# Token expansion by expert weights: all token loads and all stores on SyncE's DMA queue, the two weight loads on ScalarE's

## The chip, the cores and the metric

The kernel runs on one core of a Trainium2 chip; the chip's other cores run nothing. The metric is the device time of one execution in microseconds (us), as the median of several executions of the same program. Less is better. The profiled execution is one more run, under the hardware profiler; its page gives a span, which begins at the program's first own instruction and ends with its last, and is a little shorter than the device time of the same run.

## What is computed

Every token row of 512 floats is written twice, each time multiplied by one of that token's two weights. The expert indices are an input that the computation doesn't use.

```python
batch, seq, hidden, n_experts = 16, 1024, 512, 8      # k = 2
x_expanded = x[:, :, np.newaxis, :].repeat(k, axis=2)  # [16, 1024, 2, 512]
weights = expert_weights[..., np.newaxis]              # [16, 1024, 2, 1]
return (x_expanded * weights).astype(np.float32)
```

There are 16384 tokens, 33.55 MB of x to read, 0.13 MB of weights to read, and 67.11 MB of output to write, all float32.

## The kernel before, in words

**Tiling.** The 16384 tokens are 128 x 128: `groups = [19, 19, 18, 18, 18, 18, 18]` cuts them into seven groups of 128 x T tokens, and a partition holds T neighbouring tokens. So a group's load is one long contiguous run per partition (18 x 2048 = 36,864 bytes), and a store of 9 tokens with two products each is 9 x 4096 = 36,864 bytes per partition.

**Loads.** `load(i)` (L120) takes a buffer of `x_pool`, which has two, and starts the DMA of group i at L128. Group 0 is loaded in two DMAs (9 and 10 tokens), every other group in one. Groups 0 and 1 are loaded ahead of the loop; at the end of its iteration i the loop calls `load(i + 2)`, whose buffer is that of group i.

**Products.** A group is worked off in two halves (j = 0 and 1), each into a buffer of `o_pool`, which has three. `products` (L134) has one long VectorE instruction (L135) that multiplies up to nine tokens by both weights, and, in one half of each group, ScalarE does the two products of one further token (L148). In every group but the first it is half 0 in which ScalarE helps, in the first group half 1. Each half is followed by its store (L172). There are 14 stores, here S0 to S13; the loads are L0a, L0b, L1, L2 to L6. S(2i) and S(2i+1) are the two stores of group i.

**Weights.** The weights have to stand in `w_tile` with a token on its partition. They come in with two small DMAs (`weights_in`, L72): `raw_a`, 38 KB for groups 0 and 1, and `raw_b`, 90 KB for groups 2 to 6. TensorE transposes them twice (L87, L98) and VectorE copies the results (L92, L106). The `raw_a` chain comes ahead of the loop; that of `raw_b` stands in the loop ahead of the second half of group 0, and its last copy after that half.

**Order.** The schedule is manual: each engine executes its instructions in the order in which the program calls them, and waits come only from data and buffers. A DMA that is started from SyncE or from ScalarE is put on that engine's queue. Before, SyncE's queue (q1 in the profile) has `raw_a` and the 14 stores; ScalarE's queue (q10) has L0a, L0b, `raw_b`, L1, and then L2 to L6, each of which stands in ScalarE's program behind the ScalarE products of the group before. A store waits for its products; a load waits until the products that read its buffer are done; products wait for their load and for the store that was three stores earlier, whose buffer they take.

Of the kernel before, what the change touches and what calls it, by code (L numbers as in the profile page):

```python
# [1 line left out]

# [4 lines left out]


@with_exitstack
def kernel(  # L10
    ctx: ExitStack,
    tc: tile.TileContext,
    x: bass.AP,
    expert_indices: bass.AP,
    expert_weights: bass.AP,
    out: bass.AP,
):
    nc = tc.nc

    batch, seq, hidden = x.shape  # L20
    k = expert_weights.shape[-1]
    P = nc.NUM_PARTITIONS
    ntok = batch * seq
    assert ntok % P == 0

    f32 = mybir.dt.float32
    row = k * hidden


    groups = [19, 19, 18, 18, 18, 18, 18]  # L30
    assert sum(groups) * P == ntok
    TX = max(groups)
    TO = (TX + 1) // 2

    xf = x.rearrange("b s h -> (b s) h")
    of = out.rearrange("b s k h -> (b s) (k h)")
    wf = expert_weights.rearrange("b s k -> (b s) k")

    w_pool = ctx.enter_context(tc.tile_pool(name="w_pool", bufs=1))
    x_pool = ctx.enter_context(tc.tile_pool(name="x_pool", bufs=2))  # L40
    o_pool = ctx.enter_context(tc.tile_pool(name="o_pool", bufs=3))

    raw_pool = ctx.enter_context(tc.tile_pool(name="raw_pool", bufs=1))
    psum = ctx.enter_context(
        tc.tile_pool(name="psum", bufs=2, space=bass.MemoryType.PSUM)
    )

    w_tile = w_pool.tile([P, sum(groups) * k], f32)

    def rows(flat, done, T):  # L50
        return flat[done * P : (done + T) * P, :].rearrange("(p a) n -> p (a n)", a=T)

    B = 8
    M = P // B
    ident = w_pool.tile([P, P], f32)
    nc.gpsimd.memset(ident, 0.0)  # L59
    nc.gpsimd.affine_select(  # L60
        out=ident,
        in_=ident,
        compare_op=mybir.AluOpType.not_equal,
        fill=1.0,
        base=0,
        pattern=[[-1, P]],
        channel_multiplier=1,
    )

    def weights_in(eng, head, G, T):  # L70
        raw_tile = raw_pool.tile([G * M, B * T * k], f32, name=f"raw{T}_tile")
        eng.dma_start(  # L72
            out=raw_tile,
            in_=wf[head * P : (head + G * T) * P, :].rearrange(
                "(q a) n -> q (a n)", a=B * T
            ),
        )
        return raw_tile

    def weights_columns(raw_tile, G, T):  # L80
        n = T * k
        col_tile = raw_pool.tile([n, G * P], f32, name=f"col{T}_tile")
        cols = col_tile.rearrange("c (q r) -> c q r", r=B)
        for r0 in range(0, B, B // 2):
            up_tile = psum.tile([n, B // 2, G * M], f32)
            for r in range(B // 2):
                nc.tensor.transpose(  # L87
                    up_tile[:, r, :],
                    raw_tile[:, (r0 + r) * n : (r0 + r + 1) * n],
                    ident[: G * M, : G * M],  # L90
                )
            nc.vector.tensor_copy(  # L92
                out=cols[:, :, r0 : r0 + B // 2],
                in_=up_tile.rearrange("c r q -> c q r"),
            )
        down_tile = psum.tile([P, G * n], f32)
        for g in range(G):
            nc.tensor.transpose(  # L98
                down_tile[:, g * n : (g + 1) * n],
                col_tile[:, g * P : (g + 1) * P],  # L100
                ident[:n, :n],
            )
        return down_tile

    def weights_out(down_tile, head, G, T):
        nc.vector.tensor_copy(  # L106
            out=w_tile[:, head * k : (head + G * T) * k], in_=down_tile
        )

    ctx.enter_context(tc.manual_schedule())  # L110

    starts = [sum(groups[:i]) for i in range(len(groups))]
    loaded = []


    def halves(i):
        T = groups[i]
        return [T - T // 2, T // 2] if i else [T // 2, T - T // 2]

    def load(i):  # L120
        if i >= len(groups):
            return
        x_tile = x_pool.tile([P, TX * hidden], f32)
        loaded.append(x_tile)
        src = rows(xf, starts[i], groups[i])
        lo = 0
        for n in halves(i) if i == 0 else [groups[i]]:
            nc.scalar.dma_start(  # L128
                out=x_tile[:, lo * hidden : (lo + n) * hidden],
                in_=src[:, lo * hidden : (lo + n) * hidden],  # L130
            )
            lo += n

    def products(o_tile, x_tile, at, n, w_at, m):  # L134
        nc.vector.tensor_tensor(  # L135
            out=o_tile[:, : m * row].rearrange("p (t k h) -> p t k h", t=m, k=k),
            in0=x_tile[:, at * hidden : (at + m) * hidden]
            .rearrange("p (t h) -> p t h", t=m)
            .unsqueeze(2)
            .to_broadcast([P, m, k, hidden]),  # L140
            in1=w_tile[:, w_at : w_at + m * k]
            .rearrange("p (t k) -> p t k", t=m)
            .unsqueeze(3)
            .to_broadcast([P, m, k, hidden]),
            op=mybir.AluOpType.mult,
        )
        for c in range(m * k, n * k):
            nc.scalar.mul(  # L148
                out=o_tile[:, c * hidden : (c + 1) * hidden],
                in_=x_tile[:, (at + c // k) * hidden : (at + c // k + 1) * hidden],  # L150
                mul=w_tile[:, w_at + c : w_at + c + 1],
            )

    raw_a = weights_in(nc.sync, starts[0], 2, 19)
    load(0)
    raw_b = weights_in(nc.scalar, starts[2], 5, 18)
    load(1)
    weights_out(weights_columns(raw_a, 2, 19), starts[0], 2, 19)

    for i, T in enumerate(groups):  # L160
        x_tile = loaded[i]
        outr = rows(of, starts[i], T)
        at = 0
        for j, n in enumerate(halves(i)):
            if i == 0 and j == 1:
                down_b = weights_columns(raw_b, 5, 18)
            o_tile = o_pool.tile([P, TO * row], f32)

            alone = j == 1 and i > 0 or j == 0 and i == 0
            m = n if alone else n - 1  # L170
            products(o_tile, x_tile, at, n, (starts[i] + at) * k, m)
            nc.sync.dma_start(  # L172
                out=outr[:, at * row : (at + n) * row], in_=o_tile[:, : n * row]
            )
            at += n
        if i == 0:
            weights_out(down_b, starts[2], 5, 18)
        load(i + 2)

# [1 line left out]
_INS = ['x', 'expert_indices', 'expert_weights']  # L181
_OUTS = [((16, 1024, 2, 512), 'float32')]


# [23 lines left out]
```

## Time and profile before

| | before |
|---|---|
| device time, median of 3 runs | 240.32 us (239.97 to 240.71) |
| device time of the profiled execution | 241.2 us |
| span of the profiled execution | 239.4 us |
| bytes moved by DMA | 100.80 MB, 3312 packets |
| mean rate over the span | 421 GB/s |
| SyncE's queue q1: packets, MB, share of the 16 DMA engines' span | 2064, 67.15, 65.0% |
| ScalarE's queue q10: the same | 1248, 33.65, 33.1% |
| VectorE busy | 133.0 us (56%) |
| ScalarE busy | 10.6 us (4%) |

The profile counts DMA work in packets; a packet here is what one partition gets or gives in one DMA. There are 16 DMA engines, and the share of a queue is the time of its packets, added up over the engines, as a share of 16 times the window. In a view of a short window a packet is counted where it starts, so that the share of a very short window can be above 1. The times from issue to landing hold the waiting in the queue as well as the moving. The profile's views don't tell the 16 DMA engines apart.

### The profile page before, as it was taken

The page shows a single profiled execution, that of the slowest core. Times are in us where ns is not written, and L with a number is a line of the kernel's source. Part 1 is how long each engine was busy: PE and PEld are TensorE (multiplying, and loading weights), DVE is VectorE, ACT ScalarE, POOL GpSimd, SP SyncE. Part 2 cuts the span into 40 slices and gives each one's busy share as a digit, 9 for nine tenths or more (in the row PEclk, how much of TensorE's full clock was granted, in tenths as well). Part 3 has the DMA queues.
Part 4 walks back from the last instruction along what each step waited for, and adds up shares of the span by engine and source line. Part 5 has one row for each costly group of instructions (what it writes and reads, how often), then busy time and mean ns, then how long its engine had stood idle before and what let it go on. Part 6 is the DMA issues. An engine that isn't in the chain of part 4 may idle for free.

```text
span 239.4 us, 196 instructions
## 1 busy us (share of the span) xinstructions
PE 3.0 (1%) x23; PEld 2.3 (1%) x23; DVE 133.0 (56%) x20; ACT 10.6 (4%) x15; POOL 0.7 (0%) x6
## 2 busy tenths in 40 slices
PE   1021000000000000000000000000000000000000
PEld 1011000000000000000000000000000000000000
DVE  1499959890093088940872910789407839690000
ACT  0040020000010000100002000002000020000000
POOL 1000000000000000000000000000000000000000
DMA  7999999999999999999999999999999999999993
GB/s 268 440 444 380 449 394 474 435 416 427 406 471 450 422 419 431 450 400 468 413 437 450 394 474 413 425 462 394 468 419 425 456 400 468 413 431 456 400 468 129
DMA packets 3312, 100.80 MB, mean 421 GB/s; under 512 B 384, under 2 KB 496, under 8 KB 496
## 3 DMA queue, kind: packets, MB, share of 16 engines
q1 hardware_dynamic: 2064, 67.15, 65.0%
q10 hardware_dynamic: 1248, 33.65, 33.1%
HBM read 33.69 MB, written 67.11 MB: 421 GB/s over the span
## 4 chain that ended last, share of the span: by engine, by line
DMA 66%; DVE 24%; issue 0%; DVEq 0%; SPq 0%
DMA out_dram<-o_tile 62%; DVE o_tile L135 24%; DMA x_tile<-in_x_dram 3%; DVE col_tile L92 0%; DVEq L135 0%; SPq L172 0%
## 5 line engine op out<-in xcount | busy, mean ns | idle before, releaser
L135 DVE TENSOR_TENSOR o_tile<-x_tile,w_tile 128x9216 f32<-128x9216 f32 (+1 forms) x14 | 131.3, 9376 | 78.2 <-DMA out_dram<-o_tile 71.2
L148 ACT ACTIVATE o_tile<-x_tile,w_tile 128x512 f32<-128x512 f32 x14 | 9.3, 714 | 170.3 <-DMA out_dram<-o_tile 123.5
L92 DVE COPY col_tile<-up_tile 38x128 f32<-38x128 f32 (+1 forms) x4 | 1.4, 378 | 4.2 <-PE up_tile L87 4.2
L87 PE MATMUL up_tile<-ident,raw_tile 32*38 32x32 f32 (+1 forms) x16 | 1.8, 284 | 14.6 <-DMA raw_tile<-in_expert_weights_dram 14.6
L148 ACT ACT_TABLE_LOAD x1 | 1.3, 1283 | 15.5 <-DMA x_tile<-in_x_dram 15.5
L87 PEld LDWEIGHTS up_tile<-ident,raw_tile 32*38 32x38 f32 (+1 forms) x16 | 1.4, 134 | 14.7 <-issue 14.7
L98 PE MATMUL down_tile<-ident,col_tile 36*128 36x36 f32 (+1 forms) x7 | 1.2, 305 | 3.0 <-DVE col_tile L92 3.0
L98 PEld LDWEIGHTS down_tile<-ident,col_tile 36*128 36x128 f32 (+1 forms) x7 | 0.9, 209 | 3.4 <-DVE col_tile L92 3.4
L106 DVE COPY w_tile<-down_tile 128x76 f32<-128x76 f32 (+1 forms) x2 | 0.6, 282 | 0.5 <-PE down_tile L98 0.5
L60 POOL TENSOR_SCALAR_AFFINE_SELECT ident<-ident 128x128 f32<-128x128 f32 x1 | 0.3, 292 | 0.1
L59 POOL MEMSET ident<- 128x128 f32 x1 | 0.2, 205 | 0.3 <-POOLq L192 0.3
L192 POOL MEMSET const-bfloat16-1.0<- 128x1 bf16 x1 | 0.1, 101 | 0.0
L192 POOL MEMSET const-uint8-127<- 128x1 uint8 x1 | 0.1, 101 | 0.0
L192 POOL MEMSET const-float32-0.0<- 128x1 f32 x1 | 0.1, 98 | 0.2 <-issue 0.2
L192 POOL MEMSET const-float32-1.0<- 128x1 f32 x1 | 0.1, 98 | 0.0
## 6 DMA issues: line engine op xcount, KB each, us to landing
out_dram<-o_tile SPq DMA_DIRECT2D x12, 4608.0 KB, 35.5
x_tile<-in_x_dram ACTq DMA_DIRECT2D x5, 4608.0 KB, 26.1
out_dram<-o_tile SPq DMA_DIRECT2D x2, 5120.0 KB, 38.8
x_tile<-in_x_dram ACTq DMA_DIRECT2D x1, 4864.0 KB, 29.9
x_tile<-in_x_dram ACTq DMA_DIRECT2D x1, 2560.0 KB, 14.3
x_tile<-in_x_dram ACTq DMA_DIRECT2D x1, 2304.0 KB, 8.4
raw_tile<-in_expert_weights_dram ACTq DMA_DIRECT2D x1, 90.0 KB, 14.2
raw_tile<-in_expert_weights_dram SPq DMA_DIRECT2D x1, 38.0 KB, 2.9
```

Source lines behind the costliest of these rows:

```text
L59: nc.gpsimd.memset(ident, 0.0)
L60: nc.gpsimd.affine_select(out=ident, in_=ident, compare_op=mybir.AluOpType.not_equal, fill=1.0, base=0, pattern=[[-1, P]], channel_multipl ...
L87: nc.tensor.transpose(up_tile[:, r, :], raw_tile[:, (r0 + r) * n : (r0 + r + 1) * n], ident[: G * M, : G * M],)
L92: nc.vector.tensor_copy(out=cols[:, :, r0 : r0 + B // 2], in_=up_tile.rearrange("c r q -> c q r"),)
L98: nc.tensor.transpose(down_tile[:, g * n : (g + 1) * n], col_tile[:, g * P : (g + 1) * P], ident[:n, :n],)
L106: nc.vector.tensor_copy(out=w_tile[:, head * k : (head + G * T) * k], in_=down_tile)
L135: nc.vector.tensor_tensor(out=o_tile[:, : m * row].rearrange("p (t k h) -> p t k h", t=m, k=k), in0=x_tile[:, at * hidden : (at + m) * hidden]
L148: nc.scalar.mul(out=o_tile[:, c * hidden : (c + 1) * hidden], in_=x_tile[:, (at + c // k) * hidden : (at + c // k + 1) * hidden], mul=w_ti ...
L192: nc = _bacc.Bacc("TRN2", target_bir_lowering=False, num_devices=1)
```

## The change

Both weight loads are started from ScalarE, and `raw_b` ahead of the first token load; all token loads are started from SyncE, in whose program they stand between the stores.

```diff
@@ load(i)
         for n in halves(i) if i == 0 else [groups[i]]:
-            nc.scalar.dma_start(
+            nc.sync.dma_start(
                 out=x_tile[:, lo * hidden : (lo + n) * hidden],
                 in_=src[:, lo * hidden : (lo + n) * hidden],
             )
@@ ahead of the loop
-    raw_a = weights_in(nc.sync, starts[0], 2, 19)
+    raw_a = weights_in(nc.scalar, starts[0], 2, 19)
+    raw_b = weights_in(nc.scalar, starts[2], 5, 18)
     load(0)
-    raw_b = weights_in(nc.scalar, starts[2], 5, 18)
     load(1)
```

In the built program SyncE's queue then holds, in this order: L0a, L0b, L1, S0, S1, L2, S2, S3, L3, S4, S5, L4, S6, S7, L5, S8, S9, L6, S10, S11, S12, S13. ScalarE's queue holds `raw_a` and `raw_b` alone. The instructions of VectorE, TensorE and GpSimd stand in the order of before; ScalarE loses its token loads.

## Prediction

> **What bounds the kernel now.** I read the page's busy times first, then its DMA part and its chain.
>
> ```profile
> span 239.4 us, 196 instructions
> ...
> PE 3.0 (1%) x23; PEld 2.3 (1%) x23; DVE 133.0 (56%) x20; ACT 10.6 (4%) x15; POOL 0.7 (0%) x6
> ...
> DMA packets 3312, 100.80 MB, mean 421 GB/s; under 512 B 384, under 2 KB 496, under 8 KB 496
> ...
> q1 hardware_dynamic: 2064, 67.15, 65.0%
> q10 hardware_dynamic: 1248, 33.65, 33.1%
> ...
> DMA 66%; DVE 24%; issue 0%; DVEq 0%; SPq 0%
> ```
>
> The busiest compute engine, VectorE, has 56%; the two queues together keep the 16 DMA engines busy for 65.0 + 33.1 = 98.1% of 239.4 us, that is 234.9 us on average. The DVE share of the chain is therefore not a bound: while VectorE multiplies, DMA runs too. What the change can move is how long the 16 DMA engines take for the same 100.80 MB, and what stands ahead of and behind them.
>
> So I asked the DMA view for windows with one kind of traffic. Stores only, 188 to 234 us:
>
> ```profile
> DMA packets 607, 20.02 MB, mean 435 GB/s; under 512 B 64, under 2 KB 64, under 8 KB 64
> ...
> q1 hardware_dynamic: 607, 20.02, 100.7%
> ```
>
> 100.7% of 46 us is 46.3 us for 20.02 MB: 432 GB/s while busy. Token loads only, 5 to 13 us:
>
> ```profile
> DMA packets 192, 3.47 MB, mean 434 GB/s; under 512 B 16, under 2 KB 16, under 8 KB 16
> ...
> q10 hardware_dynamic: 192, 3.47, 100.9%
> ```
>
> 100.9% of 8 us, 8.07 us for 3.47 MB: 430 GB/s. And 33 to 188 us, where loads come and go beside stores:
>
> ```profile
> q1 hardware_dynamic: 1295, 43.48, 64.9%
> q10 hardware_dynamic: 720, 23.59, 35.3%
> ```
>
> 100.2% of 155 us is 155.3 us for 67.07 MB: 432 GB/s. The three kinds cost the same per byte, and no window leaves the engines idle. At 432 GB/s all 100.80 MB need 233.3 us, and 234.9 were used. Most of the 1.6 us too many lies in the first 30 us:
>
> ```profile
> DMA packets 608, 11.86 MB, mean 395 GB/s; under 512 B 64, under 2 KB 176, under 8 KB 176
> ...
> q10 hardware_dynamic: 512, 10.05, 81.9%
> q1 hardware_dynamic: 96, 1.81, 14.7%
> ```
>
> 96.6% of 30 us is 29.0 us, where 11.86 MB at 432 GB/s need 27.5: 1.5 us too many. The end of the span, by the windows view (last two columns: DMA share, GB/s):
>
> ```profile
> 234.00:234.50 0.50, 0.00 (x0) 0.00 (x0) 0.00 (x0) 0.00 (x0) 0.00 (x0) 1.00 0.51 221
> 234.50:235.00 0.50, 0.00 (x0) 0.00 (x0) 0.00 (x0) 0.00 (x0) 0.00 (x0) 1.00 2.22 958
> 235.00:235.50 0.50, 0.00 (x0) 0.00 (x0) 0.00 (x0) 0.00 (x0) 0.00 (x0) 1.00 0.00 0
> 235.50:236.00 0.50, 0.00 (x0) 0.00 (x0) 0.00 (x0) 0.00 (x0) 0.00 (x0) 1.00 0.18 74
> 236.00:236.50 0.50, 0.00 (x0) 0.00 (x0) 0.00 (x0) 0.00 (x0) 0.00 (x0) 1.00 0.01 0
> 236.50:237.00 0.50, 0.00 (x0) 0.00 (x0) 0.00 (x0) 0.00 (x0) 0.00 (x0) 1.00 0.17 74
> ```
>
> A store packet of 36.9 KB takes 36.9 KB / 27 GB/s = 1.36 us of one engine. 221 GB/s for half a us are three such packets, 958 are thirteen, 74 is one. So sixteen start up to 235.0, and then a single engine starts one more at 235.5 to 236 and its last at 236.5 to 237. Fifteen engines are done by 235.0 + 1.4 = 236.4; **one engine is about 2 us late**, and the kernel waits for it.
>
> **The change part by part.** All times are against the profiled execution: span 239.4 us, 1.8 us around it, 241.2 in all, 0.9 above the median of 240.32. I apply differences to the median.
>
> *Issues and their waits: 0.* The rows of before are these, from the timeline and SyncE's waits:
>
> ```profile
> 9.20 9.76 DVE L135 TENSOR_TENSOR o_tile<-x_tile,w_tile 128x9216 f32<-128x9216 f32 x1 [3.76 <-DMA x_tile<-in_x_dram]
> 18.99 10.85 SPq L172 DMA_DIRECT2D out_dram<-o_tile  x2
> 29.49 0.36 ACTq L128 DMA_DIRECT2D x_tile<-in_x_dram  x1
> 32.89 9.76 DVE L135 TENSOR_TENSOR o_tile<-x_tile,w_tile 128x9216 f32<-128x9216 f32 x1 [3.22 <-DMA x_tile<-in_x_dram]
> ...
> SPq L172 <- DVE o_tile L135: 191.7, 13, 21.4
> ```
>
> SyncE did nothing but wait for products (191.7 us of it), so eight more issues of about 0.36 us each cost nothing there. L(i+2) now stands behind S(2i+1) on SyncE, but both wait for the same products of group i: L2 went out at 29.49, with the second store. Queued behind the load is S(2i+2), whose products come some 9 us later. Where the built program makes SyncE wait for a landing, too, it lies 20 us back or more by the walk below (L3, issued near 50, waits for L1, landed near 28).
>
> *The order in the queue: 0, if it never runs dry.* In one queue the loads no longer overtake. I walk it at 432 GB/s: 10.9 us for 4.72 MB, 12.1 us for 5.24 MB. The loads ahead (9.73 MB and the weights) take 1.7 us of start, 22.8 us, and the 1.5 us above: to 26. S0 is ready at 19.0, **7 us before its turn**. It runs to 37, S1 (ready at 29.5) to 49, L2 to 60, S2 to 72, S3 to 83, L3 to 94. Group 1 has landed at about 28; its products run one after the other from 30 to 50, in time for 60. Group 2's first products start when L2 has landed, near 62, and are done at 71; they are wanted at 94. The second half takes S2's buffer, free at 74, and is done at 84, when L4 is issued, with L3, S4 and S5 (32 us of work) in the queue. This repeats every 33 us: each product stage starts on a landing and has some 20 us to spare. At the end, where no load stands between, S13 is issued about 9 us before S12 is through. Before, L1 landed at 32.9 (it shared with S0); now near 28, and nothing needs it. If the cover is gone, a gap of the queue costs its full length; it takes 7 us of delay at S0 to open the first.
>
> *`raw_b` from between L0b and L1 to the start: 0.* Around its old place, 14.1 to 15.6 us:
>
> ```profile
> DMA packets 110, 0.70 MB, mean 467 GB/s; under 512 B 26, under 2 KB 94, under 8 KB 94
> ...
> q10 hardware_dynamic: 110, 0.70, 129.3%
> ```
>
> 129.3% of 1.5 us is 1.94 us for 0.70 MB that at 432 GB/s need 1.62: 0.3 us lost around these 80 small packets. The same loss may come at their new place, beside `raw_a`. Ends: -0.3, and +0.5 if they disturb the first load as well as it is disturbed already; I take 0. That L0a lands 0.3 us later moves S0's readiness, within its 7 us.
>
> *The late engine: -2 to 0.* Does its lateness come from loads lying beside stores? In the window 33 to 188 the busy time was 155.3 us, and 67.07 MB at the stores-only rate (46.32 us for 20.02 MB) would be 155.2: 0.1 us on average over 16 engines is 2 us on one. That is just the lateness, and the stores-only window adds nothing. But a rounding of 0.1% of 155 us is as large, so the rows don't settle it. In the new order each engine has loads alone and then stores alone. I take the middle, **-1.0 us**.
>
> *Switches between loads and stores: 0 to +4.9.* One queue switches from loads to stores at S0, S2, S4, S6, S8, S10 and back at L2 to L6: eleven switches, of which before had the first. It can be seen there, 21.5 to 25 us, as sixteen load packets, one per engine:
>
> ```profile
> DMA packets 32, 1.21 MB, mean 346 GB/s; under 512 B 0, under 2 KB 0, under 8 KB 0
> ...
> q10 hardware_dynamic: 16, 0.62, 55.1%
> ```
>
> 55.1% of 3.5 us is 1.93 us per packet; a 38.9 KB packet at 27 GB/s needs 1.44: the last load packet before the first store was 0.49 us too long. On the other side, 33 to 188 us has each engine alternate between the queues (720 packets beside 1295) without loss, and the stores-only window goes through the ends of its DMAs without loss. These rows hold many more switches than the one at S0, so I take 0 and keep 10 x 0.49 = 4.9 as the upper end.
>
> The Trainium skill, "DMA: Bandwidth & Descriptors", section "Anatomy of one DMA", gives each DMA a fixed cost of about 2 us beside its data, mostly for the write's receipt; with nothing beside it in one queue, ten new boundaries would add 20 us, an estimate: 260. The stores-only window speaks against that, since its four stores in 46 us show no such gap.
>
> **Sum:** -1.0 us: span 238.4, profiled execution 240.2, median **239.3**.
>
> **The rivals.**
> 1. *Nothing moves: 240.3.* The late engine stays late for a reason of its own, and switches are free. For it: all three windows at the same rate, and DMA at 98.1% already. Against: the 0.1 us in the mixed stretch. That the change does nothing at all belongs here too. The Trainium skill says it outright, in the same page's "Issuing engines are not separate DMA queues": DMAs of all issuing engines run on the same 16 DMA engines, and another issuer saves only issue time. By that rule the time stays at 240.3.
> 2. *Slower, by switches in one queue: 242.8 to 245.2.* Before, a switch between loads and stores on an engine was one between two queues; now it is within one queue and falls on all 16 engines at about the same time, after 11 us of pure loads or 22 us of pure stores. The only such switch of before cost 0.49 us. If each later one from loads to stores costs that, 5 x 0.49 = 2.4 us, 242.8; with those back, 4.9 us, 245.2. It decides from 0.07 us per switch (0.7 us in all), and passes the gain of the sum at 0.1 us per switch.
> 3. *The late engine is quite cured: 238.3.* -2.0 us; fifteen engines' end sets the span.
>
> **How the numbers follow.** The forecast with rival 3 (the late engine is less late, switches nearly free): 0.42, of which rival 3 has a third. Rival 1: 0.30. Rival 2: 0.28, of which 0.02 for something like the 260 above. A measurement of this kernel tells about 0.3%, 0.72 us, from no change. The first case lies below 239.6, the second within 239.6 to 241.0, the third above. The range goes from 238.0 (rival 3 with `raw_b`'s 0.3) to 243.4, over the half of rival 2 in which only switches to stores cost; what is left out is the rest of it and a little below. The likeliest case's own range is 238.0 to 239.6.
>
> **What would show it.** Right: q1 holds nearly all bytes at about 98% of the span, the window of the last us shows the single packets closer behind the fifteen, and windows around S2's and L3's turn (60 and 83 us) show 432 GB/s. Rival 1: the same tail as above. Rival 2: packets before or after each switch are longer, and the mean rate falls below 421 GB/s. The working would be wrong if a slice in the middle of the span shows DMA idle: then products came too late, and VectorE's waits would be for a landing load with an empty queue behind it.

## The result, and the profile after

The changed kernel takes 241.97 us (median of 6 runs, 241.52 to 242.54); the kernel of before takes 239.74 us in six runs (239.34 to 240.71), three of which were measured beside the changed one. The ratio is 1.0087, with a 95% interval of 1.0061 to 1.0114: slower by 2.1 us, where 1.0 us less than 240.32 was forecast. The time lies within the range (238.0 to 243.4), on the wrong side. Here and below a ratio leaves out executions that are over 1.5% longer than the fastest one of their kernel; e6_mixed, m_eight and m_fine have such executions, and their medians and ranges hold them.

The page of the changed kernel, from its head, its DMA part and its chain:

```profile
span 239.8 us, 196 instructions
...
DMA  7999999999999999999999999999999999999993
...
DMA packets 3312, 100.80 MB, mean 420 GB/s; under 512 B 384, under 2 KB 496, under 8 KB 496
...
q1 hardware_dynamic: 3168, 100.66, 97.9%
q10 hardware_dynamic: 144, 0.13, 0.2%
...
DMA 65%; DVE 24%; SPq 0%; issue 0%; DVEq 0%
DMA x_tile<-in_x_dram 36%; DMA out_dram<-o_tile 30%; DVE o_tile L135 24%; DVE col_tile L92 0%; SPq L172 0%; DVEq L135 0%; SPq L128 0%
```

The change does what it says: q1 has all but the weights. The two queues' share, 98.1%, is that of before. The chain goes through loads now (36% instead of 3%), because products wait for a load that stands in line; that alone costs nothing. The span is only 0.4 us longer than the 239.4 of before, while the medians differ by 2.2 us. So the two profiles alone don't explain the result, and the first thing to find out was which of them is unusual.

The end of the span, by the windows view (last two columns: DMA share and GB/s; 74 GB/s for half a us is one packet of 36.9 KB):

```profile
234.50:235.00 0.50, 0.00 (x0) 0.00 (x0) 0.00 (x0) 0.00 (x0) 0.00 (x0) 1.00 2.22 958
235.00:235.50 0.50, 0.00 (x0) 0.00 (x0) 0.00 (x0) 0.00 (x0) 0.00 (x0) 1.00 0.51 221
235.50:236.00 0.50, 0.00 (x0) 0.00 (x0) 0.00 (x0) 0.00 (x0) 0.00 (x0) 1.00 0.17 74
236.00:236.50 0.50, 0.00 (x0) 0.00 (x0) 0.00 (x0) 0.00 (x0) 0.00 (x0) 1.00 0.18 74
236.50:237.00 0.50, 0.00 (x0) 0.00 (x0) 0.00 (x0) 0.00 (x0) 0.00 (x0) 1.00 0.17 74
237.00:237.50 0.50, 0.00 (x0) 0.00 (x0) 0.00 (x0) 0.00 (x0) 0.00 (x0) 1.00 0.17 74
```

Most engines start their last packet by 235.5, but single packets still start in each of the next four half microseconds. A packet takes 1.36 us, so one engine can't have started all four: more than one engine is late, and the last one starts its last packet between 237.0 and 237.5.

When did they get late? The products of a group start when the slowest engine has landed its load, and those of a second half when it has landed a store, so VectorE's rows are a clock of the slowest engine (start, duration, and in brackets the wait and what ended it):

```profile
61.42 8.69 DVE L135 TENSOR_TENSOR o_tile<-x_tile,w_tile 128x8192 f32<-128x8192 f32 x1 [12.11 <-DMA x_tile<-in_x_dram]
73.57 9.76 DVE L135 TENSOR_TENSOR o_tile<-x_tile,w_tile 128x9216 f32<-128x9216 f32 x1 [3.46 <-DMA out_dram<-o_tile]
95.62 8.69 DVE L135 TENSOR_TENSOR o_tile<-x_tile,w_tile 128x8192 f32<-128x8192 f32 x1 [12.29 <-DMA x_tile<-in_x_dram]
106.56 9.76 DVE L135 TENSOR_TENSOR o_tile<-x_tile,w_tile 128x9216 f32<-128x9216 f32 x1 [2.25 <-DMA out_dram<-o_tile]
128.88 8.69 DVE L135 TENSOR_TENSOR o_tile<-x_tile,w_tile 128x8192 f32<-128x8192 f32 x1 [12.56 <-DMA x_tile<-in_x_dram]
139.75 9.76 DVE L135 TENSOR_TENSOR o_tile<-x_tile,w_tile 128x9216 f32<-128x9216 f32 x1 [2.18 <-DMA out_dram<-o_tile]
162.57 8.69 DVE L135 TENSOR_TENSOR o_tile<-x_tile,w_tile 128x8192 f32<-128x8192 f32 x1 [13.06 <-DMA x_tile<-in_x_dram]
173.51 9.76 DVE L135 TENSOR_TENSOR o_tile<-x_tile,w_tile 128x9216 f32<-128x9216 f32 x1 [2.25 <-DMA out_dram<-o_tile]
195.50 8.69 DVE L135 TENSOR_TENSOR o_tile<-x_tile,w_tile 128x8192 f32<-128x8192 f32 x1 [12.23 <-DMA x_tile<-in_x_dram]
```

From S2 landed (73.57) to L3 landed (95.62) the queue moves S3 and L3, 9.44 MB, which at 432 GB/s is 21.8 us; the rows say 22.05. The same leg takes 22.3 (106.56 to 128.88), 22.8 (139.75 to 162.57) and 22.0 (173.51 to 195.50): about 1.9 us too much in four legs. The legs from a load to the next store (95.62 to 106.56, and so on) move one store, 10.9 us, and take 10.9 each. So the slowest engine loses time in the legs that end with a load, and keeps it.

The packets show it directly. These are windows of the changed kernel at the end of L5, where the queue goes over from that load to S8, and one behind it:

```profile
158.00:158.50 0.50, 0.00 (x0) 0.00 (x0) 0.00 (x0) 0.00 (x0) 0.00 (x0) 1.00 1.88 737
158.50:159.00 0.50, 0.00 (x0) 0.00 (x0) 0.00 (x0) 0.00 (x0) 0.00 (x0) 1.00 0.99 369
159.00:159.50 0.50, 0.00 (x0) 0.00 (x0) 0.00 (x0) 0.00 (x0) 0.00 (x0) 1.00 0.26 74
161.00:161.50 0.50, 0.00 (x0) 0.00 (x0) 0.00 (x0) 0.00 (x0) 0.00 (x0) 1.00 2.22 958
```

The share times half a us times 16 engines is the time of the packets that start in a row. The ten of the first row take 1.50 us each, the five of the second 1.58, the single one of the third 2.08; the thirteen store packets of the last row take the usual 1.37. So packets at this switch are longer, by 0.1 to 0.2 us on average and by 0.7 us for one that starts late. The trace's packet records say the same of the five switches behind 30 us, and of nothing else: in this profile 36 large packets are there over 0.06 us longer than their size needs, at most 0.71, and 35 of them stand at the end of L2, L3, L4, L5 or L6. Averaged over the 16 engines the loss is small: 98.1% of 239.8 us is 235.2 us of work, 0.3 us more than before.

### The profile page after: what moved, and what is told of

Its sections match the earlier page's. It is cut to its first block, busy times and chain, and to the rows that moved or that the text cites. A ratio compares the mean times of both kernels' runs of the same rounds, so it can differ in the third digit from the quotient of the medians.

```text
span 239.8 us, 196 instructions
## 1 busy us (share of the span) xinstructions
PE 3.0 (1%) x23; PEld 2.3 (1%) x23; DVE 132.8 (55%) x20; ACT 10.6 (4%) x15; POOL 0.7 (0%) x6
## 4 chain that ended last, share of the span: by engine, by line
DMA 65%; DVE 24%; SPq 0%; issue 0%; DVEq 0%
DMA x_tile<-in_x_dram 36%; DMA out_dram<-o_tile 30%; DVE o_tile L135 24%; DVE col_tile L92 0%; SPq L172 0%; DVEq L135 0%; SPq L128 0%
```

## The experiments

The theory at this point, the **switch theory**: where loads and stores stand in one queue, each switch from loads to stores costs the engines that end last some tenths of a us. Its rivals: the **start** (the weights' packets beside the first load), an **unevenness** of any single queue, **SyncE's queue** as such, and **products and waits**. Ratios are to the kernel of before, on the same chip, with 95% intervals.

**e0_before and e0_after: the two kernels once more**, unchanged.

> The kernel of before, unchanged, once more: what its time and its profile are on this chip beside the others. Ratio to before 1.000 within 0.002 by every theory. If the profile's span comes out near 238 us with the tail of its last engine shorter, the first profile of before (241.2 us in all, above the median of 239.7) was a slow sample, and the two profiles on record understate the change; if it is again near 239.4, they don't.

> The changed kernel, unchanged, once more. About 1.009 by every theory (1.0087 before). Switch theory: packets are lengthened at each switch from loads to stores (near 25, 59, 93, 126, 158 and 191 us) and hardly elsewhere behind 30 us, and the engines end more unevenly than in the kernel of before.

Measured: 239.37 us, 1.0001 (0.9979 to 1.0023), and 241.74 us, 1.0094 (1.0060 to 1.0128). The page of e0_before and its end by the windows view:

```profile
span 237.5 us, 196 instructions
...
q1 hardware_dynamic: 2064, 67.15, 65.5%
q10 hardware_dynamic: 1248, 33.65, 33.4%
```

```profile
234.50:235.00 0.50, 0.00 (x0) 0.00 (x0) 0.00 (x0) 0.00 (x0) 0.00 (x0) 1.00 2.39 1032
235.00:235.50 0.50, 0.00 (x0) 0.00 (x0) 0.00 (x0) 0.00 (x0) 0.00 (x0) 1.00 0.34 147
235.50:236.00 0.50, 0.00 (x0) 0.00 (x0) 0.00 (x0) 0.00 (x0) 0.00 (x0) 1.00 0.00 0
```

Here no engine is late: 98.9% of 237.5 us is the same 234.9 us of work as before, and the span is 1.9 us shorter because all engines end together. So the late engine of the first profile (241.2 us, above all six runs) is not there in every execution of that kernel. Some others are as long, 241.15 us among the twelve here; whether by a late engine too isn't shown. e0_after's span is 239.1 us, in the shortest of its six executions. Against a usual execution of before, the changed kernel loses 1.6 us in this pair of profiles and 2.4 us in the medians.

**e1_start and e2_late: the change in two halves.** e1 takes the new place of the weights, and L0 and L1 on SyncE; e2 takes only L2 to L6 on SyncE.

```diff
 # e1_start, against the changed kernel
-            nc.sync.dma_start(
+            (nc.sync if i < 2 else nc.scalar).dma_start(
 # e2_late, against the kernel of before
-            nc.scalar.dma_start(
+            (nc.scalar if i < 2 else nc.sync).dma_start(
```

> The start of the changed kernel alone: both weight loads on ScalarE ahead of everything, L0 and L1 on SyncE, but L2 to L6 on ScalarE as before. Switch theory (each later switch between loads and stores in one queue costs): only the first switch is in one queue, so the time is that of before, ratio 0.998 to 1.002. Start theory (the small weight packets beside the first load, and S0 behind L1): all of the loss, 1.007 to 1.011. Lateness theory (any engine with all traffic in one queue gets uneven by itself): 0.998 to 1.002.

> The rest of the changed kernel alone: weights, L0 and L1 as before, but L2 to L6 on SyncE between the stores. Switch theory: nearly all of the loss, ratio 1.006 to 1.011. Start theory: 0.998 to 1.002. Lateness theory: 1.006 to 1.011, with lengthened packets anywhere and not at the switches.

Measured: e1 240.46 us, 1.0039 (1.0008 to 1.0069); e2 242.11 us, 1.0100 (1.0066 to 1.0134). The later loads alone bring the whole loss. e1 is outside what the switch theory gave it, by a little: the first half of the change has a small price of its own, which doesn't add up with the other. The ends of e1 and of e2 by the windows view show two different things:

```profile
235.00:235.50 0.50, 0.00 (x0) 0.00 (x0) 0.00 (x0) 0.00 (x0) 0.00 (x0) 1.00 1.36 590
235.50:236.00 0.50, 0.00 (x0) 0.00 (x0) 0.00 (x0) 0.00 (x0) 0.00 (x0) 1.00 0.68 295
236.00:236.50 0.50, 0.00 (x0) 0.00 (x0) 0.00 (x0) 0.00 (x0) 0.00 (x0) 1.00 0.01 0
```

```profile
236.00:236.50 0.50, 0.00 (x0) 0.00 (x0) 0.00 (x0) 0.00 (x0) 0.00 (x0) 1.00 0.35 148
236.50:237.00 0.50, 0.00 (x0) 0.00 (x0) 0.00 (x0) 0.00 (x0) 0.00 (x0) 1.00 0.17 74
237.00:237.50 0.50, 0.00 (x0) 0.00 (x0) 0.00 (x0) 0.00 (x0) 0.00 (x0) 1.00 0.00 0
237.50:238.00 0.50, 0.00 (x0) 0.00 (x0) 0.00 (x0) 0.00 (x0) 0.00 (x0) 1.00 0.34 147
```

In e1 (first) twelve packets start from 235 to 236: most engines are half a us later than in e0_before, and none trails. In e2 (second) two single engines start their last packet at 237.5 to 238, and the rest are done: the changed kernel's tail.

Where e1's half us goes, the DMA view tells for 30 to 45 us of e1 (first two lines) and of e0_before:

```profile
q1 hardware_dynamic: 104, 3.28, 50.6%
q10 hardware_dynamic: 77, 2.84, 47.7%
q1 hardware_dynamic: 112, 3.60, 55.6%
q10 hardware_dynamic: 96, 2.95, 45.5%
```

In e1 98.3% of 15 us, 14.75 us, move 6.12 MB, which at 432 GB/s need 14.17: 0.6 us too much, where e0_before needs just its 15.2. The first 30 us, with the weights, cost both the same (96.9% and 97.2% for 11.86 MB). So e1's price isn't one of the weights' new place; it comes while L2, in the other queue, runs beside stores, and why is not shown.

**e3_six and e4_eleven: more switches, the same bytes.** Loads are cut in halves with buffers of their own; e3 issues both halves behind the second store, e4 one behind each store.

```diff
 # e4_eleven, against e3_six
             at += n
+            load(i + 2, (j,))
         if i == 0:
             weights_out(down_b, starts[2], 5, 18)
-        load(i + 2)
```

> The changed kernel with each load cut in two DMAs into two smaller buffers, both issued where the one was: still six switches from loads to stores. Switch theory and run-length theory: the time of the changed kernel, ratio to before 1.007 to 1.012. It is the base for the next run.

> As the run before, but the first half of each load stands behind the first store of the group and the second half behind the second store: eleven switches from loads to stores in the one queue, each after half as long a run of loads. Switch theory with a fixed price (2.3 us over six switches, about 0.4 us each on the engine that ends last): 2 us more than with six, ratio to before 1.015 to 1.020. Run-length theory (the price goes with the length of the run of loads ahead of the switch): as with six, 1.007 to 1.012, or less if short runs cost nothing.

Measured: e3 241.53 us, 1.0083 (1.0049 to 1.0116), as the changed kernel; e4 243.30 us, 1.0154 (1.0112 to 1.0197). Five more switches cost 1.8 us, 0.35 us each, though each run of loads is half as long. The two intervals just touch, so the price per switch is a rough one. The switch theory's number came out; that the price goes with the length of a run did not.

**e5_swap: the issuers exchanged.** Two queues as before, but loads on SyncE and stores on ScalarE.

```diff
 # against the kernel of before: token loads and raw_b
-nc.scalar.dma_start(
+nc.sync.dma_start(
 # stores and raw_a
-nc.sync.dma_start(
+nc.scalar.dma_start(
```

> Two queues as in the kernel of before, with their issuers exchanged: token loads and the second weight load on SyncE, stores and the first weight load on ScalarE. Switch theory (it is loads and stores in the same queue that costs, not which engine issues them): ratio to before 0.997 to 1.003. Rival (loads cost more when SyncE issues them): 1.006 to 1.012.

Measured: 239.58 us, 0.9986 (0.9958 to 1.0014). Loads on SyncE cost nothing as long as the stores are elsewhere. SyncE's queue as such is ruled out.

**m_one and m_two: without weights and products.** The output isn't computed: stores send a zeroed tile.

```diff
+    nc.vector.memset(o_tile, 0.0)
-    products(...); weights_in(...); weights_columns(...); weights_out(...)
 # m_two, against m_one: the loads
-            nc.sync.dma_start(
+            nc.scalar.dma_start(
```

> No weights and no products: the output is not computed, all stores send the same zeroed tile, and the loaded tokens are not used. All loads and stores in SyncE's queue in the order of the changed kernel. Switch and run-length theory: packets are lengthened at the six switches as in the changed kernel, and the time is 1.5 to 3 us above that of the next run. Rival (products, waits and the vector engine's traffic make the difference): the same as the next run within 0.7 us.

> As the run before without weights and products, but with the loads in ScalarE's queue and the stores in SyncE's, as in the kernel of before. All theories: no lengthened packets after the first switch; 236 to 239.5 us. Its distance from the run before is what tells.

Measured: m_one 241.94 us, 1.0093 (1.0068 to 1.0118): the changed kernel's time with no product and no weight in it. So products, their waits and VectorE's traffic aren't needed for the loss. m_two, meant as its base, took 248.81 us, 1.0379 (1.0334 to 1.0424), against every expectation. With no products to wait for, its first store goes out at 11.6 us (19.0 in the kernel of before), its loads run beside stores from then on, and its page-wide rate fell to 407 GB/s. Its packets take 96.6% of 247.3 us, 238.9 us, 4 us more than in e0_before, and single packets still start between 240 and 245 us. So the distance between the two tells nothing, and loads beside stores in two queues aren't free in every order; why not in this one stays open.

**m_eight and m_fine: 8 switches and 64.** Again without weights and products; every DMA has two tokens per partition, all in SyncE's queue.

```diff
 # m_fine, against m_eight
         for c in range(b, b + 8):
             load(c)
-        for c in range(b, b + 8):
             store(c)
```

> No weights and no products, as in the earlier runs of that kind (output not computed, stores send zeros). One queue, every DMA cut to two tokens per partition: eight loads, then eight stores, eight times over: eight switches from loads to stores, fewer loads per run than in the changed kernel. It is the base of the next run: 238 to 246 us, as small packets cost something of their own.

> The same DMAs as the run before in the order load, store, load, store: 64 switches from loads to stores. Fixed price per switch of the engine that ends last (0.3 to 0.4 us, from six against eleven): 17 to 22 us above the run before. If the price needs a run of some length, or all engines going over from loads alone to stores alone: at most 2 us above, or below.

Measured: 249.62 us (246.35 to 250.04), 1.0408 (1.0358 to 1.0458), and 260.90 us (255.78 to 262.31), without a ratio. m_eight missed its 238 to 246: its 16,384 packets of 4 and 8 KB take 99.8% of 244.6 us, 9 us more than the packets of e0_before. Most of the 11.3 us between the two, or of the 9.4 us between their shortest executions, is a slip of mine: in m_fine the second DMA is a store that waits for the zeroed tile, with all loads but one behind it. The rates of the first three slices of each page (m_eight's slices are 6.1 us, m_fine's 6.5) are 251, 415, 423 and 81, 41, 355 GB/s; against 425 throughout, 186 GB/s x 6.1 us = 1.1 MB and 798 GB/s x 6.5 us = 5.2 MB are missing, 2.6 and 12.1 us: some 9.5 us more in m_fine. Between nothing and 2 us are left for 56 more switches. A fixed price of 0.3 to 0.4 us per switch is ruled out for such short runs; between six and eleven it held. So neither count nor length alone sets the price.

**e6_mixed: every second store in the other queue.**

```diff
 # against the changed kernel
-            nc.sync.dma_start(
+            (nc.scalar if j else nc.sync).dma_start(
                 out=outr[:, at * row : (at + n) * row], in_=o_tile[:, : n * row]
```

> The changed kernel, but the second store of every group goes to ScalarE's queue; loads and first stores stay together in SyncE's. SyncE's queue still switches from loads to stores six times, but the other queue mostly has stores beside it. If a switch costs because the 16 engines go over from loads alone to stores alone: 0.998 to 1.003, no lengthened packets after the first. If the switch within a queue costs as such: 1.005 to 1.011.

Measured: 252.30 us (247.52 to 258.43), 1.0331 (1.0267 to 1.0395). Both expectations missed by far: spreading the stores over both queues makes the loss nearly four times as large. But the run doesn't test the switch. The profiled execution, the longest of the six, has its queues run dry; three windows and a row of VectorE:

```profile
230.00:235.00 5.00, 0.00 (x0) 0.00 (x0) 1.26 (x1) 0.00 (x0) 0.00 (x0) 1.00 0.14 59
235.00:240.00 5.00, 0.00 (x0) 0.00 (x0) 5.00 (x1) 0.00 (x0) 0.00 (x0) 1.00 0.07 29
240.00:245.00 5.00, 0.00 (x0) 0.00 (x0) 3.50 (x1) 0.00 (x0) 0.00 (x0) 1.00 0.27 118
233.74 9.76 DVE L135 TENSOR_TENSOR o_tile<-x_tile,w_tile 128x9216 f32<-128x9216 f32 x1 [17.02 <-DMA out_dram<-o_tile]
```

The last products wait 17.02 us for a store whose buffer they take. By 230 us little else is left to move, and DMA is all but idle until the products are done and the last store can go. In all, packets take 61.6 + 30.9 = 92.5% of 256.7 us, 237.5 us, only 2.6 us more than in e0_before. The rest of this execution's loss is DMA standing idle. Whether the two executions of the ratio, 8 us above the kernel of before, lose their time so too is not shown.

**e7 to e10: one engine made late on purpose.** The packet records of the changed kernel, chained by their starts and ends, suggested that engines that come late to a switch have their last load packet lengthened most. No view tells the engines apart, so this was to be tried: a small DMA that is meant to fall to one engine alone, at the start, in the changed kernel (e7, e9) and in that of before (e8, e10).

```diff
 # e7_delay_after and e8_delay_before (e8 on nc.sync)
+    late_tile = raw_pool.tile([31, 64], f32)
+    nc.scalar.dma_start(out=late_tile, in_=xf[:31, :64])
 # e9_delay3_after and e10_delay3_before (e10 on nc.sync)
+    late_tile = raw_pool.tile([19, 1024], f32)
+    nc.scalar.dma_start(out=late_tile, in_=xf.rearrange("(a b) h -> a (b h)", b=2)[:19, :])
```

> The changed kernel with one more small DMA at the start (31 partitions of 256 bytes, on ScalarE's queue behind the weights, its data unused), so that one engine enters the first switch about 1.6 us behind the others. Late-engine theory (who comes late to a switch pays about 0.5 to 0.8 us there, so lateness grows): that engine ends 1.6 + 5 or 6 times 0.6 to 0.8, 4.5 to 6.5 us late, time 243.5 to 246, ratio to before 1.017 to 1.028. Rival (the price falls on engines whatever their lateness): at most the 1.6 us more than the changed kernel if the same engine is hit, usually less: 241.5 to 243.3, ratio 1.008 to 1.016.

> The kernel of before with the same small DMA at the start, on SyncE's queue behind the first weights. Late-engine theory: loads and stores lie in two queues, there are no switches, the lateness stays what it is: 1.0 to 1.8 us above before, ratio 1.004 to 1.008. If it grows here too (ratio above 1.012), the lateness feeds on something other than the switches in one queue.

Measured: e7 242.68 us, 1.0111 (1.0076 to 1.0145); e8 241.01 us, 1.0067 (1.0037 to 1.0098). By the packet records the small packets took 18 ns each, a third of what I had assumed, so the pair decides nothing.

> The changed kernel with one more DMA at the start (19 partitions of 4096 bytes, data unused, on ScalarE's queue behind the weights), 3 us of one engine. Late-engine theory: that engine pays 0.5 to 0.8 us at each of six switches on top of its 3 us and ends 6 to 8 us behind; ratio to before 1.023 to 1.033. Rival (the price falls on engines whatever their lateness): the worse of 3 us and the 2.3 us of the changed kernel, or both on one engine at most: 1.011 to 1.022.

> The kernel of before with the same DMA at the start, on SyncE's queue behind the first weights. Late-engine theory and rival: the 3 us stay 3 us, less what the scatter hides: ratio 1.009 to 1.014. Above 1.018 the lateness grows without switches in one queue, and the theory is wrong as it stands.

Measured: e9 244.13 us, 1.0176 (1.0147 to 1.0204), in the rival's range and below the theory's 1.023; e10 243.21 us, 1.0150 (1.0119 to 1.0181), above the 1.014 given to both. The lateness doesn't grow as I had it. VectorE's rows of e9 still show where the late engine loses:

```profile
76.68 9.76 DVE L135 TENSOR_TENSOR o_tile<-x_tile,w_tile 128x9216 f32<-128x9216 f32 x1 [3.33 <-DMA out_dram<-o_tile]
98.92 8.69 DVE L135 TENSOR_TENSOR o_tile<-x_tile,w_tile 128x8192 f32<-128x8192 f32 x1 [12.48 <-DMA x_tile<-in_x_dram]
109.84 9.76 DVE L135 TENSOR_TENSOR o_tile<-x_tile,w_tile 128x9216 f32<-128x9216 f32 x1 [2.23 <-DMA out_dram<-o_tile]
132.11 8.69 DVE L135 TENSOR_TENSOR o_tile<-x_tile,w_tile 128x8192 f32<-128x8192 f32 x1 [12.51 <-DMA x_tile<-in_x_dram]
143.03 9.76 DVE L135 TENSOR_TENSOR o_tile<-x_tile,w_tile 128x9216 f32<-128x9216 f32 x1 [2.23 <-DMA out_dram<-o_tile]
165.36 8.69 DVE L135 TENSOR_TENSOR o_tile<-x_tile,w_tile 128x8192 f32<-128x8192 f32 x1 [12.57 <-DMA x_tile<-in_x_dram]
```

The legs of a store and a load take 22.2, 22.3 and 22.3 us where 21.8 would do: 0.4 to 0.5 us lost at each, while the landing of e9's S2 is 3.1 us behind that of the changed kernel (76.68 against 73.57). An engine that is 3 us late pays about 0.45 us per switch, no more than one that is late by less. That the late engine pays is in keeping with this; that the price grows with lateness is not.

**Settled:** the loss comes from the later loads' sharing a queue with the stores; not mainly from the first half of the change (whose own part is 0.1 to 0.7%), not from SyncE, not from products or waits, and not from an unevenness elsewhere in the queue. It is lost in the legs from a store to the end of the next load, by a few engines, in pieces of up to 1.0 us. **Open:** what makes a switch long on one engine; whether it takes one queue, or only that engines go over from loads alone to stores, as at S0 of the kernel of before, where loads went on in the other queue; and why m_two, with two queues, is slow too. No version beat the kernel of before; e5 equals it.

## Why the prediction was wrong

- *What bounds the kernel* was right: DMA at 98%, and the last engine sets the end.
- *Issues and their waits, 0; the order in the queue, 0 if it never runs dry:* right. The walk had group 2's products at 62, the second half at 74 and L3 at 94; the rows have 61.42, 73.57 and 95.62 for the three landings. No slice between the first and the last shows DMA idle.
- *`raw_b` to the start, 0 within -0.3 and +0.5:* right as far as the profiles show, though it wasn't tried alone. The first 30 us of the changed kernel have DMA busy for 96.1% with 11.86 MB (94.8 + 1.3), those of before for 96.6% with the same; its first products start at 9.50 us instead of 9.20, well within the slack of S0. The 0.9 us that e1 lost (0.2 to 1.7) lie behind 30 us.
- *The late engine, -1.0:* **this step failed first.** It took the 2 us of one execution for a property of the kernel. The profiled run's 241.2 us stood above all runs shown then, and that was the sign: e0_before shows the usual execution without a late engine (span 237.5). There was nothing to gain, and the new order didn't cure lateness but made it: in the changed kernel more than one engine ends late.
- *Switches, 0 within 0 to +4.9:* **this step failed as well, and it set the sign.** I weighed many free alternations between two queues, and boundaries between stores in one, against the single switch that looked like the new ones, and took the many. They were another case: two queues that each go on, against one queue in which loads end and stores begin. The measured price is 2.1 to 2.4 us over the five new switches from loads to stores, 0.4 to 0.5 us each, or 0.35 by e4 against e3; the row at S0 had 0.49. Rival 2 named the step and, with 242.8 for the switches to stores alone, came within 0.8 us, though it had the price fall on all 16 engines, where the packets show it on a few. It is owing to this rival that the range held the time; the sum pointed the other way.
- The Trainium skill's "Issuing engines are not separate DMA queues" (page "DMA: Bandwidth & Descriptors") would have left the time as it was. e5 agrees with it as far as the issuing engine goes (0.9986); the result doesn't (1.0087), since not the issuer but the mix within a queue changed. The fixed cost per DMA of that page's "Anatomy of one DMA", a section on DMAs that GpSimd issues, would by the prediction's estimate have given 260 and isn't there: the legs of two DMAs lose 0.2 to 1.0 us, those of one store nothing.

## What to carry to other kernels

A DMA-bound kernel at 98% busy can still lose or gain at its tail: ask whether a single engine ends last, and whether it does so in more than one execution; a profile above the median of the runs is a poor base for a sum. Here long loads and long stores did better in separate queues, whichever engine issued them; m_two shows that separate queues alone don't ensure it. Take a price seen once in just the new situation over a nought seen often in another.

## What the runs showed of the hardware

A kernel with the token loads, stores and queues of before but no products to wait for (m_two) was 9 us slower than it: loads beside stores are not always free. Where the queue went over from a load to a store (end of L5), one load packet of 36.9 KB took 2.08 us instead of 1.36. Adding 31 packets of 256 bytes made the kernel of before 1.6 us slower (1.0067), adding 19 of 4096 bytes 3.6 us (1.0150).
